# Modulation products in four row bands of one bank, late transposes of the last token tiles, and a moved norm in a two-layer hybrid step

## The chip, the cores and the metric

The kernel runs on one core of a Trainium2 chip. The metric is the device time of one execution in microseconds (us). One profiled execution gives the page and the trace; three executions give the median.

## The reference

One inference step of a two-layer trunk over 128 context tokens and 512 latent tokens, width 1024. Both groups use the same weights, and each has a conditioning vector of its own (c_ctx and c). Layer 0 mixes tokens by grouped-query attention and a gated delta rule side by side, layer 1 by a Mamba-2 scan. The frame around them is this:

```
mod = silu(cond) @ w_mod[layer] + b_mod[layer]           # 1024 -> 6 x 1024, for both vectors
sh1, sc1, g1, sh2, sc2, g2 = split(mod, 6)
h = rms_norm(x) * norm_mix_g * (1 + sc1) + sh1
y, state = even_mixer(h) if layer == 0 else odd_mixer(h)
x = x + g1 * y
h = rms_norm(x) * norm_mlp_g * (1 + sc2) + sh2
x = x + g2 * (max(h @ w_mlp_in, 0) ** 2) @ w_mlp_out
...
return rms_norm(x) * final_norm_g                         # after both layers; also the new caches and states
```

The modulation is a product of a 1024 x 6144 matrix per layer with only two vectors. In odd_mixer the scan's result is normalised over its 2048 channels (rms_norm with a gain) before the output product.

## The kernel before

The 640 tokens are five tiles of 128: tile 0 is the context, tiles 1 to 4 are latent. A product in full precision is made of three products of split operands (high x high, high x low, low x high), so each weight tile that lands raw is cast to a high part (ScalarE) and a low part (VectorE). `gemm` (L304) gives channels on partitions: 24 matmuls accumulate in a bank. `by_rows` (L330) gives tokens on partitions, in two halves (hm) of 512 output columns; the second half holds its last weights back and finishes one token tile after another, calling done(t) after each.

**Modulation.** Shift and scale of layer 0's mixer come first (`mod_first`, product at L515): the weights' 512 columns are cut in four, and four matmuls of 128 columns write to the partitions 0 to 31, 32 to 63, 64 to 95 and 96 to 127 of one bank. The other 20 blocks of 512 columns go through the generator `mod_steps`: it loads a raw tile of 1 MB (two per block, L469) and works on the tile that was loaded one step earlier, so that a caller takes a step wherever it wants one.

- Blocks 4 to 9 of layer 0 (gate g1, shift sh2, scale sc2) run in `delta_in` of the first delta head, three steps ahead of each of four convolution products (12 steps of work). Each k multiplies the [128, 32] window `condst` (the two vectors in columns 0 and 1, zeros behind) by 512 columns into rows 0 to 31 of the bank (L462).
- The other 14 blocks (g2 of layer 0 and all of layer 1) run as `side` of the first MLP: VectorE and ScalarE form the weighted sums in two `macc` tiles (L486, L489), and TensorE adds over the partitions with two products against a selector `msel`, again through L462.

At the end of each block `mod_out` adds the bias to two rows (L444), for some blocks applies 1 + scale and the gain, and writes the rows to a table `modr` in memory, from which `bands` later reads them broadcast to all partitions. `mod_bias` loads the bias and gain rows of each block through SP's queue.

**Norm and transposes.** `modulated` works while the second half of `by_rows` finishes its tiles. Its squares go to ScalarE; done(1), done(2) and done(4) take the root for the tiles that are ready and make the scaled rows `hrow` (L402, L403); `turned` transposes four 128 x 128 pieces of a row tile into a bank (L409) and splits the result into high and low parts (ScalarE L412, VectorE L413). After tile 4, done makes all the transposes that are left, so that in the program they stand ahead of the products that follow: the first `stage` of an MLP, or the scan's first products (`odd`). `stage` takes pairs of weight blocks, and for each half of the tokens (hf) runs four gemms, one for each of four weight tiles j. hf = 0 reads token tiles 0, 1 and the first half of 2.

**The scan's norm.** In `odd` 15 products against the column `stat` (`stc`, L1413) sum the squares of the scan's result, VectorE makes the root `yr`, and the eviction of the output products (`gated`, L365) multiplies by it. These products stand ahead of the output products.

Each engine works through its own queue in order. The order in a queue follows the program where nothing else is said, and the framework may place an instruction later or earlier by a plan of its own (in the trace some products pass transposes that stand ahead of them in the program). Loads of weights go through SP's queue in one sequence.

Of the kernel before, what the change touches and what calls it, by code (L numbers as in the profile page):

```python
# [11 lines left out]
F32 = mybir.dt.float32  # L12
# [99 lines left out]
def _rows(i):  # L112

    out, index, pos = [], {}, 0

    def put(key, v):
        nonlocal pos
        index[key] = pos
        out.append(np.asarray(v).reshape(-1))
        pos += out[-1].size  # L120

    for layer in range(2):
        for c in range(12):
            put(("bias", layer, c), np.stack([i["b_mod"][layer, c * 512:c * 512 + 512]] * 2))
        for c in (2, 3, 8, 9):
            gain = i["norm_mix_g" if c < 4 else "norm_mlp_g"][layer]
            put(("gain", layer, c), np.stack([gain[c % 2 * 512:c % 2 * 512 + 512]] * 2))
    put("gfin", i["final_norm_g"])
    return np.concatenate(out), index
# [36 lines left out]
def _consts():  # L166
# [11 lines left out]
    put("ident", np.eye(P))  # L178
    put("stat", np.full((P, 1), 1.0 / 32.0))
# [28 lines left out]
class Prog:  # L208
    def __init__(self, nc, tc, ctx, io, widx, ridx, pidx, cidx, csmall, taps=None):
        self.nc, self.tc, self.ctx, self.io = nc, tc, ctx, io  # L210
        self.turn, self.share = 0, False
        self.behind = None
        self.mlast = None
        self.widx, self.ridx, self.pidx, self.cidx, self.csmall = widx, ridx, pidx, cidx, csmall
        self.taps = taps or {}
# [91 lines left out]
    def stage(self, keys, xs, half, evac, side=None):  # L307

        for i in range(0, len(keys), 2):
# [9 lines left out]
    def by_rows(self, keys, parts, evac, done=None, side=None, pre=()):  # L319
# [12 lines left out]
        for hm in range(2):  # L332
            banks, held = [], []
            for i, key in enumerate(keys(hm)):
# [3 lines left out]
                for j in range(2):  # L338
# [51 lines left out]
    def modulated(self, pool, scale, shift, h, off, halves):  # L390
# [24 lines left out]
        def done(t):  # L415
# [15 lines left out]
    def mod_bias(self, layer, c, pool):  # L431

        out = []
        for key in ("bias", "gain")[:2 if (layer, c) in self.gains else 1]:
            x = pool.tile([2, 512], F32, name=f"m{key}", tag=f"m{key}", bufs=2 if key == "bias" else 1)
            o = self.ridx[key, layer, c]
            self.nc.sync.dma_start(out=x, in_=self.io["rows"][o:o + 1024].rearrange("(p x) -> p x", p=2))
            out.append(x)
        return out

    def mod_out(self, layer, c, ps, row, gain=None):

        nc = self.nc
        nc.vector.tensor_tensor(out=row, in0=ps[0:2], in1=row, op=ALU.add)  # L444
        if gain is not None:
            nc.vector.scalar_tensor_tensor(out=row, in0=row, scalar=1.0, in1=gain, op0=ALU.add, op1=ALU.mult)
        nc.scalar.dma_start(out=self.modr[layer][c // 2, :, c % 2 * 512:c % 2 * 512 + 512], in_=row)

    def mod_steps(self, todo, landing, small, pool=None, after=None):
# [4 lines left out]
        if pool:  # L454
            sel = pool.tile([P, 2, 32], F32, name="msel")
            nc.vector.memset(sel, 0.0)
            for j in range(2):
                nc.vector.memset(sel[:, j, j:j + 1], 1.0)
        raws, n = [], 2 * len(todo)
# [1333 lines left out]
```

## Time and profile before

| what | value |
|---|---|
| median of 3 runs | 2224.25 us (2221.36 to 2229.6) |
| the profiled execution | 2224.19 us, of which the span of the trace is 2222.4 us |
| TensorE (PE) busy | 2112.9 us, 95% of the span |
| VectorE (DVE) busy | 1386.5 us, 62% |
| ScalarE (ACT) busy | 897.9 us, 40% |
| GpSimd (POOL) busy | 151.1 us, 7% |
| DMA | 232.97 MB, mean 105 GB/s |

Busy time of an engine is an average over stages with different limits. The rows further down are from four views: the page of the whole execution; windows, which give each engine's busy time, the granted TensorE clock (PEclk, 1.00 is 2.4 GHz and 0.50 is 1.2 GHz) and the DMA's share for a stretch; the chain of waits that ended last; and the timeline of one engine. L462 is line 462 of the kernel before, PEld is TensorE's weight load, and x8 means that eight instructions stand in one entry. A product of f32 operands is two instructions in the trace.

### The profile page before, as it was taken

The page shows a single profiled execution, that of the slowest core. Times are in us where ns is not written, and L with a number is a line of the kernel's source. Part 1 is how long each engine was busy: PE and PEld are TensorE (multiplying, and loading weights), DVE is VectorE, ACT ScalarE, POOL GpSimd, SP SyncE. Part 2 cuts the span into 40 slices and gives each one's busy share as a digit, 9 for nine tenths or more (in the row PEclk, how much of TensorE's full clock was granted, in tenths as well). Part 3 has the DMA queues.
Part 4 walks back from the last instruction along what each step waited for, and adds up shares of the span by engine and source line. Part 5 has one row for each costly group of instructions (what it writes and reads, how often), then busy time and mean ns, then how long its engine had stood idle before and what let it go on. Part 6 is the DMA issues. An engine that isn't in the chain of part 4 may idle for free.

```text
span 2222.4 us, 32146 instructions
## 1 busy us (share of the span) xinstructions
PE 2112.9 (95%) x12883; PEld 1851.6 (83%) x12883; DVE 1386.5 (62%) x2606; ACT 897.9 (40%) x1892; POOL 151.1 (7%) x112
## 2 busy tenths in 40 slices
PE   6999789998989999999889999999989799999998
PEld 5958687786787888889789999999968698989896
DVE  6355676766589767574667877777642644444445
ACT  4324435345243322313237876667532231313131
POOL 1031220300000000000000101111210000000000
PEclk9999889999999999999989999999989899999999
DMA  7251100004245434332214443333342121212221
GB/s 316 95 190 64 37 1 17 18 1 149 93 152 211 168 133 145 122 133 79 88 46 151 146 145 115 127 119 113 111 173 83 67 95 57 89 63 81 72 76 48
DMA packets 55152, 232.97 MB, mean 105 GB/s; under 512 B 6487, under 2 KB 20799, under 8 KB 33115
## 3 DMA queue, kind: packets, MB, share of 16 engines
q1 hardware_dynamic: 45192, 216.34, 27.6%
q10 hardware_dynamic: 9810, 14.58, 1.9%
q8 instruction: 101, 1.65, 0.3%
q14 instruction: 49, 0.39, 0.1%
HBM read 222.47 MB, written 8.43 MB: 104 GB/s over the span
## 4 chain that ended last, share of the span: by engine, by line
PE 90%; DVE 5%; DMA 2%; ACT 2%; issue 1%; POOL 0%; SPq 0%; DVEq 0%; ACTq 0%; POOLq 0%
PE gps L304 42%; PE rps L330 28%; PE modps L462 3%; PE yps L1695 2%; PE atps L749 2%; PE avps L1326 2%; PE offps L1709 1%; PE stps L1726 1%; DMA X<-growd 1%; PE scps L1268 1%; DMA wraw<-wall 1%; PE dps L1027 1%; PE dps L1033 1%; PE xkps L1545 1%; PE hps L409 1%
## 5 line engine op out<-in xcount | busy, mean ns | idle before, releaser
L304 PE MATMUL gps<-hh,whi 128*128 128x322 f32 (+3 forms) x1552 | 492.4, 318 | 3.3 <-ACT whi L276 2.6
L304 PE MATMUL gps<-hl,whi 128*128 128x322 f32 (+3 forms) x1552 | 487.0, 314 | 0.0
L304 PE MATMUL gps<-hh,wlo 128*128 128x322 f32 (+3 forms) x1552 | 486.0, 314 | 0.0
L304 PEld LDWEIGHTS gps<-hh,whi 128*128 128x128 f32 (+1 forms) x1552 | 293.5, 189 | 18.4 <-issue 7.6
L304 PEld LDWEIGHTS gps<-hl,whi 128*128 128x128 f32 (+1 forms) x1552 | 293.4, 189 | 6.5 <-issue 5.9
L304 PEld LDWEIGHTS gps<-hh,wlo 128*128 128x128 f32 (+1 forms) x1552 | 293.0, 189 | 3.2 <-issue 2.5
L330 PE MATMUL rps<-wlo,hidh 128*128 128x512 f32 x640 | 253.0, 395 | 0.0
L330 PE MATMUL rps<-whi,hidh 128*128 128x512 f32 x640 | 252.3, 396 | 0.0
L330 PE MATMUL rps<-whi,hidl 128*128 128x512 f32 x640 | 251.5, 395 | 0.0
L276 ACT CAST whi<-wraw 128x1024 fp32r<-128x1024 f32 (+2 forms) x132 | 140.0, 1062 | 259.0 <-PE rps L330 178.9
L304 PE MATMUL gps<-yh,whi 128*128 128x320 f32 x1024 | 227.6, 311 | 1.4 <-DVE yh L413 1.4
L288 DVE TENSOR_TENSOR wlo<-wraw,whi 128x1024 fp32r<-128x1024 f32 x88 | 108.9, 1240 | 189.8 <-ACT whi L287 189.7
L279 DVE TENSOR_TENSOR wlo<-wraw,whi 128x1024 fp32r<-128x1024 f32 (+3 forms) x123 | 156.8, 1276 | 106.4 <-ACT whi L276 105.7
L287 ACT CAST whi<-wraw 128x1024 fp32r<-128x1024 f32 x88 | 91.7, 1048 | 276.2 <-PE rps L330 199.3
L304 PEld LDWEIGHTS gps<-yh,whi 128*128 128x128 f32 x1024 | 173.3, 190 | 2.1 <-DVE yh L413 1.8
L304 PE MATMUL gps<-yh,wlo 128*128 128x320 f32 x512 | 159.3, 311 | 0.0
L330 PEld LDWEIGHTS rps<-whi,hidh 128*128 128x128 f32 x640 | 120.2, 188 | 33.4 <-ACT macc L489 4.2
L330 PEld LDWEIGHTS rps<-whi,hidl 128*128 128x128 f32 x640 | 120.2, 188 | 29.0
L330 PEld LDWEIGHTS rps<-wlo,hidh 128*128 128x128 f32 x640 | 120.3, 188 | 28.5
L649 DVE TENSOR_SCALAR hr<-gps 128x320 f32<-128x320 f32 x128 | 62.4, 488 | 119.9 <-PE gps L304 119.9
L486 DVE SCALAR_TENSOR_TENSOR macc<-wraw,condst,macc 128x512 f32<-128x512 f32 x196 | 136.3, 737 | 0.9 <-DMA wraw<-wall 0.7
L650 ACT ACTIVATE hr<-hr 128x320 f32<-128x320 f32 x128 | 59.9, 469 | 166.8 <-DVE hr L649 166.8
(428 smaller groups left out, 3629.7 us busy)
## 6 DMA issues: line engine op xcount, KB each, us to landing
wraw<-wall SPq DMA_DIRECT2D x158, 1024.0 KB
bc<-afs SPq DMA_DIRECT2D x40, 512.0 KB
Q<-afr SPq DMA_DIRECT2D x64, 128.0 KB
xt<-xt ACTq DMA_DIRECT2D x1, 2560.0 KB
X<-growd SPq DMA_DIRECT2D x8, 320.0 KB
x<-x ACTq DMA_DIRECT2D x1, 2560.0 KB
xd<-x ACTq DMA_DIRECT2D x1, 2560.0 KB
x<-xd SPq DMA_DIRECT2D x1, 2560.0 KB
```

Source lines behind the costliest of these rows:

```text
L276: self.nc.scalar.copy(out=hi, in_=raw[:, :, c:c + m])
L279: eng.tensor_tensor(out=lo, in0=raw[:, :, c:c + m], in1=hi.bitcast(F32), op=ALU.subtract)
L287: self.nc.scalar.copy(out=hi, in_=x)
L288: self.nc.vector.tensor_tensor(out=lo, in0=x, in1=hi.bitcast(F32), op=ALU.subtract)
L304: self.nc.tensor.matmul(ps, ws[k // KT][q // 2][:, k % KT, :], xs[q % 2][k][:, c], start=k == 0 and q == 0, stop=k == n - 1 and q == 2)
L330: nc.tensor.matmul(ps, parts[x][k][:, c], w[y][:, j, :], start=k == 0 and q == 0, stop=k == n - 1 and q == 2)
L462: nc.tensor.matmul(ps, lhs, x, start=start, stop=stop)
L486: nc.vector.scalar_tensor_tensor(out=a, in0=x, scalar=w, in1=a, op0=ALU.mult, op1=ALU.add)
L649: nc.vector.tensor_scalar(out=r, in0=ps, scalar1=0.0, scalar2=None, op0=ALU.max)
L650: nc.scalar.activation(out=r, in_=r, func=AF.Square)
L749: nc.tensor.matmul(ps[:, :n], x[k][:, TOFF[t]:TOFF[t] + P], w[:, k, :], start=k == 0 and q == 0, stop=k == KT - 1 and q == 2)
L1326: nc.tensor.matmul(acc, val(c, i), p, start=c == 1, stop=c == 6)
```

## The change

- **Products side by side.** `mod_steps` cuts the 512 columns in four as `mod_first` does: four products of 128 columns to four groups of 32 partitions. `condst` has the two vectors in columns 32 and 34 of 64, and the window that a block takes of it puts its results into rows of its own. All blocks of a group therefore add up in one bank: a group starts it once and stops it once. The groups are chunks 2 to 4 of layer 0, chunk 5 of layer 0, and all six chunks of layer 1.
- **One way out per group.** `mod_out` runs once per group: an add of the bias, a multiplication by the gains, and four DMAs on ScalarE's queue. The `band` array (bias and gain in the bank's layout) is loaded once per group in place of the rows of each block. `macc` has one buffer for each of its two tiles.
- **Late transposes.** done(4) keeps the transposes of tiles 3 and 4. `stage` makes them after the products j = 1 (one), 2 (one) and 3 (two) of its first pair's first half; the scan makes all four after its first three products, in banks of `ps_x`. `hrow` moves to the weight pool with four buffers. In the even layer the shift rows lie in four tiles that the delta heads used, filled by four loads.
- **The scan's norm.** The 15 products and the root become `mid`, which `by_rows` calls after the products of its first half and ahead of their evictions.
- The final norm's gain is an input array of its own.

```diff
@@ by_rows, stage
             for hf in range(2):
                 for j, w in enumerate(tiles):
                     evac(2 * i + j, hf, self.gemm(w, xs, hf, half))
+                    if i == hf == 0:
+                        self.late((0, 1, 1, 2)[j])
...
+            if mid and not hm:
+                mid()
             for t in range(NT):
                 ps = banks[t] if banks else self.pg.tile([P, 512], F32, name="rps", tag="g")
@@ modulated
-                y = halves(t, j)
+                y = self.wp.tile([P, 512], F32, name="hrow", tag="hrow", bufs=4)
...
-                v.tensor_tensor(out=y, in0=y, in1=shift[:, q, c], op=ALU.add)
+                v.tensor_tensor(out=y, in0=y, in1=shift(q, j), op=ALU.add)
...
-            ps = self.pn.tile([P, 512], F32, name="hps", tag="n")
+            ps = self.bank("hps")
...
-            if t == 4:
-                while todo:
-                    turned(*todo.pop(0))
+            self.turns = todo, turned
...
+    def late(self, n):
+
+        todo, turned = self.turns
+        for _ in range(min(n, len(todo))):
+            turned(*todo.pop(0))
+
+
+    def mod_out(self, layer, chunks, ps, band):
+
+        v = self.nc.vector
+        t = self.small.tile([P, P], F32, name="modt", tag="modt")
+        v.tensor_tensor(out=t, in0=ps, in1=band[:, :P], op=ALU.add)
+        v.scalar_tensor_tensor(out=t, in0=t, scalar=self.cst("scales"), in1=band[:, P:], op0=ALU.add, op1=ALU.mult)
+        r = slice(4 * chunks[0], 4 * chunks[-1] + 4)
+        for q in range(4):
+            self.nc.scalar.dma_start(out=self.modr[layer].rearrange("a b (h q c) -> q (a b h) c", h=2, q=4)[q, r], in_=t[32 * q + r.start:32 * q + r.stop])
@@ mod_steps
         def product(lhs, x, start, stop):
-            nc.tensor.matmul(ps, lhs, x, start=start, stop=stop)
+            for q in range(4):
+                nc.tensor.matmul(ps[32 * q:32 * q + 32], lhs, x[:, q * P:(q + 1) * P], start=start, stop=stop)
...
-                if i % 2 == 0:
-                    nextrows = self.mod_bias(layer, c, small)
...
+                    if first:
+                        ps = self.pmod.tile([P, 512], F32, name="modps", tag="mod")[:, :P]
+                        band = small.tile([P, 2 * P], F32, name="band", tag="band")
+                        nc.sync.dma_start(out=band, in_=self.io["band"][layer])
+                    acc = [pool.tile([P, 512], F32, name="macc", tag=f"macc{j}") for j in range(2)] if pool else []
...
-                        product(self.condst[:, k, :], x, k == 0, k == KT - 1)
+                        product(self.condst[:, k, 32 - row:64 - row], x, first and k == 0, last and k == KT - 1)
...
-                        product(sel[:, j], a, j == 0, j == 1)
-                    self.mod_out(layer, c, ps, *rows)
+                        r = row + 2 * j
+                        product(sel[:, 32 - r:64 - r], a, first and j == 0, last and j == 1)
+                    if last:
+                        self.mod_out(layer, cs, ps, band)
@@ even
-        shift = self.bands(np_.tile([P, 2, D], F32, name="shift"), 0, 3)
+        shift = {}
+        for n, tag in enumerate(("dq1", "dq2", "dq3", "dz3")):
+            q, j = divmod(n, 2)
+            shift[q, j] = ev2.tile([P, PC], F32, name="shift", tag=tag)[:, :512]
+            nc.sync.dma_start(out=shift[q, j], in_=self.modr[0][3, q:q + 1, j * 512:j * 512 + 512].to_broadcast([P, 512]))
@@ odd
             first = [(x, self.gemm(x, xs, 0, HP, cols=CCUT[0])) for x in w]
+            self.bank = lambda name: self.ps_x.tile([P, 512], F32, name=name, tag="x")
+            self.late(4)
...
+            def mid():
+
+                pc = self.bank("stc")
+                for t in range(NT):
+                    for j, y in enumerate([ysq] + sq):
+                        nc.tensor.matmul(pc[:, t:t + 1], y[:, t * P:(t + 1) * P], self.cst("stat"), start=j == 0, stop=j == 2)
...
+            self.by_rows(lambda hm: [("outo", hm, kq) for kq in range(4)], (hh, hl), evac, done, pre=pre, mid=mid)
```

## Rows read from the trace of the kernel before

**Rows 1.** The page, busy time by engine and the chain by engine.

```profile
PE 2112.9 (95%) x12883; PEld 1851.6 (83%) x12883; DVE 1386.5 (62%) x2606; ACT 897.9 (40%) x1892; POOL 151.1 (7%) x112
...
PE 90%; DVE 5%; DMA 2%; ACT 2%; issue 1%; POOL 0%; SPq 0%; DVEq 0%; ACTq 0%; POOLq 0%
```

**Rows 2.** Windows: us, busy us (instructions) by engine, PEclk, DMA share, GB/s.

```profile
28.60:30.50 1.90, 1.90 (x37) 1.39 (x29) 1.90 (x7) 1.90 (x6) 0.00 (x0) 0.50 1.01 418
36.70:38.70 2.00, 2.00 (x67) 1.79 (x66) 1.66 (x12) 0.00 (x0) 0.00 (x0) 1.00 1.02 426
100.00:180.00 80.00, 80.00 (x345) 44.60 (x344) 49.73 (x97) 22.07 (x64) 18.11 (x18) 1.00 0.44 159
110.00:131.00 21.00, 21.00 (x92) 12.38 (x91) 18.13 (x27) 3.85 (x7) 10.99 (x10) 1.00 0.53 188
632.00:1100.00 468.00, 468.00 (x2488) 399.49 (x2487) 326.17 (x514) 144.63 (x237) 0.00 (x0) 1.00 0.38 135
546.00:556.00 10.00, 5.88 (x17) 4.64 (x18) 8.28 (x11) 5.24 (x6) 0.00 (x0) 0.57 0.78 306
1126.00:1132.00 6.00, 5.96 (x23) 4.87 (x24) 2.21 (x2) 1.13 (x3) 0.00 (x0) 0.55 0.41 147
1633.00:1637.00 4.00, 4.00 (x12) 3.14 (x11) 3.94 (x6) 1.04 (x1) 1.56 (x1) 0.57 0.38 162
```

**Rows 3.** The chain of waits: start us, us, engine and line, instructions.

```profile
102.55 3.55 PE modps L462 x8
106.10 1.98 PE gps L304 x12
...
111.62 3.88 PE gps L304 x25
...
743.51 1.83 PE modps L462 x4
...
1628.83 3.02 PE stc L1413 x28
```

**Rows 4.** Timeline of PE, opening: start us, us, engine, line, operation, tiles [idle before].

```profile
28.62 1.93 PE L515 MATMUL modps<-wraw,condst 128*32 128x128 f32 x32
...
36.75 1.95 PE L515 MATMUL modps<-wraw,condst 128*32 128x128 f32 x64
```

**Rows 5.** The chain of waits at a weight load, 1612 to 1620 us.

```profile
1613.45 4.99 DMA wraw<-wall
```

**Rows 6.** Timeline of PE at the first head's transposes.

```profile
139.12 0.27 PE L865 MATMUL kvps<-con,dq 128*128 128x128 f32 x1
```

**Rows 7.** Timeline of DVE, 110 to 131 us.

```profile
111.66 0.68 DVE L444 TENSOR_TENSOR mbias<-modps,mbias 2x512 f32<-2x512 f32 x1 [0.76 <-PE modps L462]
...
130.23 0.82 DVE L678 SCALAR_TENSOR_TENSOR vt<-cb,vt 128x642 f32<-128x642 f32 x1
```

**Rows 8.** Timeline of PE at a wait in the even layer's output products.

```profile
550.12 2.50 PE L330 MATMUL rps<-whi,op 128*128 128x512 f32 x5 [4.19 <-ACT whi L287]
```

**Rows 9.** Timeline of PE ahead of the second MLP.

```profile
1747.78 1.94 PE L409 MATMUL hps<-con,hrow 128*128 128x128 f32 x8 [7.12 <-DVE hrow L403]
...
1754.47 1.94 PE L409 MATMUL hps<-con,hrow 128*128 128x128 f32 x8 [4.75 <-DVE hrow L403]
...
1760.32 0.90 PE L304 MATMUL gps<-yh,whi 128*128 128x320 f32 x2 [1.40 <-DVE yh L413]
```

**Rows 10.** Timeline of DVE ahead of the second MLP.

```profile
1750.31 0.16 DVE L243 SCALAR_TENSOR_TENSOR nr<-rsa,nr 128x2 f32<-128x2 f32 x1
1750.39 0.68 DVE L413 TENSOR_TENSOR yh<-hps,yh 128x512 fp32r<-128x512 f32 x1
```

**Rows 11.** Timeline of PE ahead of the scan.

```profile
1123.59 0.66 PE L409 MATMUL hps<-con,hrow 128*128 128x128 f32 x4 [1.40 <-DVE hl L413]
...
1125.87 0.64 PE L304 MATMUL gps<-hh,whi 128*128 128x322 f32 x1 [1.62 <-ACT whi L276]
```

**Rows 12.** Timeline of DVE at the evictions of the odd layer's output products.

```profile
1680.74 1.45 DVE L365 SCALAR_TENSOR_TENSOR rps<-rps,yr,gate 128x512 f32<-128x512 f32 x2 [1.85 <-PE rps L330]
```

More of the change, by code (lines that the diff above doesn't have):

```diff
@@ L109, in _stream, with _bands, band @@
     return np.concatenate(out), index
[L112 to L129, printed above, removed]
+def _bands(i):
+    def band(rows):
+        x = np.stack(rows, axis=0).reshape(6, 2, 4, P)
+        o = np.zeros((4, 8, 2, 2, P), np.float32)
+        o[:, :6] = x.transpose(2, 0, 1, 3)[:, :, None]
+        return o.reshape(P, P)
+    one = np.ones(D, np.float32)
+    return np.stack([np.concatenate([
+        band(list(i["b_mod"][layer].reshape(6, D))),
+        band([one, i["norm_mix_g"][layer], one, one, i["norm_mlp_g"][layer], one])], axis=1) for layer in range(2)])
 def _params(i):
@@ L388, in norm_rows, with modulated @@
         return square, root
-    def modulated(self, pool, scale, shift, h, off, halves):
+    def modulated(self, pool, scale, shift, h, off):
         nc, v = self.nc, self.nc.vector
@@ L535, in setup @@
         self.modr = [self.dr.tile([6, 2, D], F32, name=f"modr{l}") for l in range(2)]
-        self.gains = {(l, c) for l in range(2) for c in (2, 3, 8, 9)}
         npr = self.io["prm"].shape[1]
@@ L795, in even @@
         np_, self.pn, self.pg = self.pools(e1, ("mn0", 1, "left"), ("pn1", 2, None), ("pg2", 6, None))
+        self.bank = lambda name: self.pn.tile([P, 512], F32, name=name, tag="n")
         h = [hp.tile([P, KT, PC], F32R, name=n) for n in ("hh", "hl")]
@@ L818, in even @@
                 e1, ("on0", 1, "right"), ("hid0", 1, "left"), ("mraw", 2, "left"), ("pn2", 1, None), ("pmod2", 1, None), ("pg3", 6, None))
-            side = self.mod_steps([(0, 10), (0, 11)] + [(1, c) for c in range(12)], mraw, np_, hid, lambda: self.mlast)
+            side = self.mod_steps([(0, (5,)), (1, range(6))], mraw, np_, hid, lambda: self.mlast)
             next(side)
@@ L827, in late @@
                 self.padding(np_, h)
-                square, done = self.modulated(np_, scale, shift, h, TOFF, lambda t, j: hid.tile([P, 512], F32, name="hrow", tag="macc", bufs=4))
+                square, done = self.modulated(np_, scale, lambda q, j: shift[:, q, j * 512:j * 512 + 512], h, TOFF)
                 sq.append(square)
@@ L1388, in odd @@
             self.pn, self.pg, np_ = self.pools(e1, ("pn3", 2, None), ("pg5", 6, None), ("on1", 1, "right"))
+            self.bank = lambda name: self.pn.tile([P, 512], F32, name=name, tag="n")
             sq = [np_.tile([P, NTOK], F32, name="ysq", tag=f"ysq{j}") for j in range(2)]
@@ L1408, in odd @@
                     nc.vector.scalar_tensor_tensor(out=hl[k], in0=y, scalar=sc, in1=hh[k].bitcast(F32), op0=ALU.mult, op1=ALU.subtract)
-            pc = self.pn.tile([P, 512], F32, name="stc", tag="n")
-            for t in range(NT):
-                for j, y in enumerate([ysq] + sq):
-                    nc.tensor.matmul(pc[:, t:t + 1], y[:, t * P:(t + 1) * P], self.cst("stat"), start=j == 0, stop=j == 2)
-            ym, yr = (np_.tile([P, NT], F32, name=n, tag=n) for n in ("ym", "yr"))
-            nc.vector.tensor_scalar(out=ym, in0=pc[:, :NT], scalar1=16.0 / D, scalar2=EPS, op0=ALU.mult, op1=ALU.add)
-            self.rsqrt(np_, yr, ym, [P, NT])
             self.x = xp.tile([P, NT, D], F32, name="x")
@@ L1420, in odd @@
             shift, scale = (self.bands(np_.tile([P, 2, D], F32, name=f"band{kind}"), 1, kind) for kind in (3, 4))
-            square, done = self.modulated(np_, scale, shift, h, [P * t for t in range(NT)],
-                                          lambda t, j: np_.tile([P, 512], F32, name="hrow", tag="hrow", bufs=4))
+            square, done = self.modulated(np_, scale, lambda q, j: shift[:, q, j * 512:j * 512 + 512], h, [P * t for t in range(NT)])
             def evac(t, hm, ps):
@@ L1762, in prepare @@
     arrays = {
-        "wall": wall, "rows": rows, "prm": prm, "cst": cst,
+        "wall": wall, "gfin": i["final_norm_g"], "band": _bands(i), "prm": prm, "cst": cst,
         "x": x.reshape(NT, P, D).transpose(1, 0, 2),
```

66 lines of the change are left out of this document (26 added, 40 removed).

## The prediction

> **What bounds the kernel now.** I read the page first, then the windows, then the chain, then the timeline of single engines. The page says TensorE: it is busy for 95% of the span and holds 90% of the chain that ended last [rows 1]. The windows say where it is the bound without a gap: in 100 to 180 us and in 632 to 1100 us its busy time equals the length of the stretch, at full clock, while VectorE has room [rows 2]. Any TensorE work taken out of these two stretches should come off the end, as long as nothing else is close behind. The chain then shows what sits between the wide products there: the modulation's products, eight instructions of 3.55 us at a time in the delta stage and four of 1.83 us in the MLP [rows 3]. Where TensorE does stand idle I read the timeline of TensorE and VectorE around the gap.
>
> The profiled execution took 2224.19 us with a span of 2222.4 us; the median of three is 2224.25 us. I work from 2224.2 us, so the 1.8 us around the span stays.
>
> **Part 1, products side by side.** Before, a block's product is a [128, 32] stationary operand against 512 columns, two instructions each. The chain's x8 and x4 are one step of the delta stage, which has 12, and one block of the MLP, which has 14 [rows 3]. After, each becomes four products of 128 columns, one per 32 partitions of the bank. The opening of this kernel already runs that form: at the full level (2.4 GHz) 64 instructions take 1.95 us, 0.030 us each, and at the half level (1.2 GHz) 32 take 1.93 us, 0.060 us each [rows 2, 4]. A 512-column instruction takes 3.55/8 = 0.444 us. Four 128-column ones in 0.12 us mean the four quarters really overlap.
> - Delta stage: a step becomes 32 instructions, 32 x 0.030 = 0.97 us, plus 0.1 us that I allow for entering and leaving (an estimate). It saves 3.55 - 1.07 = 2.48 us, times 12 = 29.8 us of TensorE time.
> - MLP: a block becomes 16 instructions, 0.48 + 0.1 = 0.58 us for 1.83, so 1.25 us times 14 = 17.5 us.
>
> A rule speaks against this. The Trainium skill (TensorE: Matmul & The Clock Gate, "Wait — 56ns, not 53.3ns?") says that without hardware decode the sequencer spends about 62 ns per matmul. By that a step of 32 would take 1.98 us and a block of 16 0.99 us, and the sum below would end near 2184 us. The full-level row has 30 ns, so the trace doesn't bear the rule out for this form; what it would do is rival 3.
>
> **What of the 29.8 us arrives.** Three things could wait once TensorE is faster.
> (a) The raw weights. Tile i+2 is requested when step i ends; its step starts after two runs of wide products and one step, 1.98 + 1.07 + 3.88 = 6.9 us [rows 3]. A 1 MB load took 4.99 us from issue to use [rows 5]. So it stays hidden, by 1.9 us.
> (b) VectorE's in-order queue. TensorE transposes the first head's q, k and v at 139.12 us [rows 6]. The last of its inputs, vt, comes from VectorE at 130.23 + 0.82 = 131.05 us [rows 7]. VectorE has been busy for 18.13 of the 21 us up to there [rows 2], mostly with the attention's preparation, which doesn't get shorter; it loses only two mbias adds of about 0.7 us and a wait of 0.76 us [rows 7], about 2.1 us. So vt is ready at 128.9. Six steps lie ahead of the transposes, so TensorE arrives at 139.1 - 6 x 2.48 = 124.2 and waits 4.7 us, if the order of its queue stays.
> (c) The clock. Around an idle time of 4.19 us the mean granted clock of 10 us was 0.57, with 5.88 us of work in them [rows 2, 8]. The waiting itself I have counted; the work after it runs at half speed, so a wait of this size would cost about another 2.7 us (half of some 5.4 us of work).
> Net: 29.8 - 4.7 - 2.7 = 22.4 us. The bounds are 29.8 (the queue is arranged around the wait) and 7.5 (the second six steps, 14.9 us, are given back as well).
>
> In the MLP VectorE is busy 326 of 468 us [rows 2] and 14 blocks in 468 us leave 33 us for each one's sums; I take all 17.5 us, at the least 14 (three blocks' gain lost at the ends of the four hidden blocks). That the accumulators (macc) have one buffer each instead of two sets costs nothing: the step that issues a block's product comes before the one that starts the next block's sums in the program, so the new write waits for a product that takes 0.6 us.
>
> Writing out once per group and not per block removes 17 of 20 small adds of 0.68 us [rows 7] and 17 bias loads, and turns 20 writes into 12. All of it is off TensorE, so nothing for the sum. It adds a wait: the two band loads of layer 1 now need the group's last product and stand in SP's queue ahead of weight loads. The bands are first needed in the last row products of the MLP; SP loses a few us, under the cover of tiles already landed. I count 0, at most +5.
>
> **Part 2, the last tiles' transposes.** Three places.
> - Before the first MLP: TensorE waits for tile 2, as before the second (below). The change doesn't touch tile 2, and in the timeline the products already pass tiles 3 and 4 here. 0, with 3 us either way because VectorE's order may change.
> - Before the second MLP: the same 7.12 us for tile 2 stays. But here the products come only after tiles 3 and 4: waits of 4.75 and 1.40 us, and transposes of eight instructions in 1.94 us, until 1760.32 [rows 9]. Tile 2's last half is ready at 1750.39 + 0.68 = 1751.1 [rows 10]. So products can start 9.2 us earlier; the 16 transposes come back between them. At full clock eight may take half of 1.94 us, about 1 us (an estimate; no row has them alone at that level), but part of that lies in gaps of wide products; net gain 8 us, between 0 (the order stays) and 9.
> - Before the scan: two waits of 1.40 us, of which the second is shown, and one of 1.62 us at the last tiles go [rows 11], and with them the half level that follows (mean clock 0.55 over 6 us, about 2.7 us of work) [rows 2]: 7.1 us. The last of these waits is for the weights' cast, and its memory may be that of the bands that tile 4 still reads; I take off 1 us. Gain 6 us, between 0 and 10.
>
> **Part 3, the scan's norm behind the products.** At the start it frees 3.02 us [rows 3] and a half level after it, 1.7 us of work (mean 0.57 over 4 us, all of them busy) [rows 2]: 4.7 us. It returns behind the first half's products: 15 sums of two instructions, as long as before, 3.0 us; then VectorE makes the root, 12 operations, 0.16 us each for two columns [rows 10] and 0.2 us for five with the steps between them (an estimate), 2.4 us, and only then can it evict: 0.73 us (1.45 for two) [rows 12] and an add that takes 0.68 us [rows 10], 1.4 us per tile. TensorE has one free bank, five tiles at 0.7 us, and waits for four evictions behind the root: 2.4 + 4 x 1.4 - 4 x 0.7 = 5.2 us. Before, the first eviction overlapped the last products. Net +3.7, rounded to a loss of 4 us, between -5 (the sums slip into gaps) and +10 (the half level follows).
>
> The shift rows now come by four loads into tiles of the delta heads, so two of them wait for the last head. If SP held the first output weights behind them, 4 to 8 us would be lost; I count 0, as the framework may issue the loads in another order.
>
> **Sum.** 2224.2 - 22.4 - 17.5 - 8 - 6 + 4 = 2174.3 us; forecast 2174.
>
> **The rivals.**
> 1. The delta stage gives back the second half as well, to waits on VectorE and the attention's start: 14.9 us less gain, 2189. For it: what releases the attention's start is not TensorE alone, and a queue in program order moves a wait on rather than ending it. Against: over the whole of 100 to 180 us VectorE has 30 us free, most of them after 131 us [rows 2]. 0.2.
> 2. Everything carries: no wait at the transposes (7.4 us more) and the norm costs nothing but its own time or less (6 us): 2161. For it: the timeline shows products passing what isn't ready. 0.2.
> 3. The narrow instructions are bound by their number and cost 0.060 us each, as in the half-level row [rows 4], because weight loads between wide products hold them up. A step takes 1.93 + 0.1 us and saves 1.52, times 12 = 18.2; a block takes 0.97 + 0.1 and saves 0.76, times 14 = 10.6; the lead at the transposes is 6 x 1.52 = 9.1 us, about what vt allows. 2224.2 - 18.2 - 10.6 - 8 - 6 + 4 = 2185. Against: the full-level row [rows 4]. 0.05. The Trainium skill's rule of part 1 is of this kind.
> 4. Slower than before: the raw tiles come too late at each of the 12 steps, as weight loads share the queue. It decides from a load of about 6.9 us. If every step then waited 4 us and the clock fell each time (another 2.6 us), that would be 12 x 6.6 = 79 us against the 29.8 us of shorter work: 2224.2 + 79 - 29.8 - 17.5 - 8 - 6 + 4 = 2246. Against: the load of 4.99 us. 0.03.
> 5. The gains of parts 2 and 3 cancel and part 1 is hardly seen, within 0.5%: 0.02.
>
> **How the numbers follow.** The forecast has 0.5. The range has to hold rivals 1 to 3 in part: rival 2 and a little below gives 2158, rival 1 and a little above 2193. A measurement of this kernel tells about 0.5% (11 us) from no change; every case but the last two is faster by more. Faster 0.94, same 0.03, slower 0.03.
>
> **What would show it.** Steps of 32 modulation instructions at about 1.05 us, blocks of 16 at 0.6 us; a TensorE wait on VectorE near the first head's transposes; no waits for hrow between the 7 us gap and the second MLP's products; a new wait for VectorE in the middle of the odd layer's output products, about 1640 us into the span. Wrong would be: steps near 2 us (rival 3), TensorE waiting for raw tiles in the delta stage (rival 4), or other stages, which the change doesn't touch, moving by more than 5 us.

## The result and the profile after

The changed kernel takes 2153.2 us (median of 4 runs, 2148.23 to 2154.41) where the kernel before takes 2226.93 us (4 runs, 2221.36 to 2236.16): a ratio of 0.9661, 95% interval 0.9623 to 0.9698. That is 74 us, where 50 us were forecast, and 5 us below the low end of the range. The profiled execution took 2148.23 us with a span of 2146.4 us, 76.0 us less than the one before.

The page of the changed kernel, beside [rows 1]:

```profile
PE 2054.9 (96%) x13339; PEld 1846.3 (86%) x13339; DVE 1373.3 (64%) x2585; ACT 898.4 (42%) x1892; POOL 153.4 (7%) x112
...
PE 89%; DVE 7%; DMA 3%; ACT 1%; issue 1%; DVEq 0%; SPq 0%; ACTq 0%
```

TensorE lost 58.0 us of busy time (2112.9 to 2054.9) and the span 76.0 us, so 18 us of idle time went as well. It is still the bound.

Where the time went is read by pairing: each VectorE and ScalarE instruction whose name stands equally often in two traces is compared with its namesake of the same number, and the median of the differences in a stretch says how far ahead the one kernel is there. The steps of that lead, in us against the profiled execution before (a plus is a gain; the kernels in the last three columns are explained below; each entry is rounded by itself, so a column can miss its sum by 0.1):

| stage (us in the kernel before) | forecast | changed | e_side | no_late | no_mid |
|---|---|---|---|---|---|
| opening (0 to 95) | 0 | +1.2 | -0.1 | +0.9 | +1.1 |
| delta stage (95 to 210) | +22.4 | +29.1 | +29.1 | +29.1 | +29.1 |
| delta heads and attention, to the first output products (210 to 580) | 0 | +7.5 | +4.1 | +7.2 | +7.5 |
| first MLP (580 to 1075) | +17.5 | +16.6 | +18.9 | +18.3 | +16.5 |
| to the end of the scan (1075 to 1535) | +6 | +6.6 | -2.3 | +3.6 | +7.5 |
| output products of layer 1 (1535 to 1720) | -4 | +5.6 | +0.7 | +6.3 | +4.1 |
| to the second MLP (1720 to 1850) | +8 | +9.6 | +2.8 | +0.1 | +9.9 |
| sum | 49.9 | 76.1 | 53.2 | 65.5 | 75.7 |

The attention's entry moves by itself: a repeat of the changed kernel has +9.9 us there in place of +7.5, and the eight traces in which TensorE's order there is that of the changed kernel have +4.1 to +10.0 (the last section). In the other stages the repeat differs from the first trace by 1.2 us at most.

So three terms are off: the delta stage by 6.7 us, the attention by 7.5 us, the output products of layer 1 by 9.6 us. The other four are right within 2 us.

In the delta stage, the timeline of TensorE in the changed kernel (start, duration, line, operation, count, idle time before and its releaser):

```profile
117.48 1.08 PE L459 MATMUL modps<-wraw,condst 128*32 128x128 f32 x32
...
121.65 0.27 PE L870 MATMUL kvps<-con,dq 128*128 128x128 f32 x1
121.76 0.27 PE L870 MATMUL kvps<-con,kt 128*128 128x128 f32 x1
...
124.21 1.08 PE L459 MATMUL modps<-wraw,condst 128*32 128x128 f32 x32 [0.54 <-DMA wraw<-wall]
...
126.75 1.08 PE L459 MATMUL modps<-wraw,condst 128*32 128x128 f32 x32
128.51 0.44 PE L870 MATMUL kvps<-con,vt 128*128 128x128 f32 x2 [0.68 <-DVE vt L679]
```

VectorE's last operation on vt:

```profile
127.31 1.14 DVE L679 SCALAR_TENSOR_TENSOR vt<-cb,vt 128x642 f32<-128x642 f32 x1
```

A step takes 1.08 us (3.55 before, [rows 3]). vt is ready at 127.31 + 1.14 = 128.45 us, near the forecast's 128.9, but the wait for it is 0.68 us and not 4.7: the queue was laid out anew. In the kernel before the transposes of q, k and v stand together (q's are in [rows 6], v's follow 0.2 us later); here q and k go from 121.4 us on, and two modulation steps, some wide products and transposes of the attention's keys fill the time until vt is there.

In the output products of layer 1, TensorE and VectorE behind the first half's products:

```profile
1613.71 2.73 PE L1436 MATMUL stc<-con,ysq 128*128 128x1 f32 x24
...
1623.69 0.50 PE L328 MATMUL rps<-whi,yh 128*128 128x512 f32 x1 [0.17 <-ACT rps L381]
```

```profile
1616.48 0.17 DVE L1437 TENSOR_SCALAR ym<-stc 128x5 f32<-128x5 f32 x1 [0.27 <-PE stc L1436]
...
1618.90 3.39 DVE L365 SCALAR_TENSOR_TENSOR rps<-rps,yr,gate 128x512 f32<-128x512 f32 x5
1622.21 3.07 DVE L366 TENSOR_TENSOR x<-x,rps 128x512 f32<-128x512 f32 x5
```

The root takes 2.4 us and the evictions follow, as forecast. But TensorE idles 0.17 us and not 5.2: in the one free bank it runs 30 products of the second half for a single tile, one k after the other (some 7 us), before it turns to the next tile.

Ahead of the second MLP (against [rows 9]) the first wide product comes straight behind tile 2's transposes:

```profile
1681.35 1.94 PE L409 MATMUL hps<-con,hrow 128*128 128x128 f32 x8 [7.12 <-DVE hrow L403]
1683.11 1.70 PE L300 MATMUL gps<-yh,whi 128*128 128x320 f32 x5
```

### The profile page after: what moved, and what is told of

It is laid out like the page before. It is cut to its first block, busy times and chain, and to the rows that moved or that the text cites. A ratio compares the mean times of both kernels' runs of the same rounds, so it can differ in the third digit from the quotient of the medians.

```text
span 2146.4 us, 32954 instructions
## 1 busy us (share of the span) xinstructions
PE 2054.9 (96%) x13339; PEld 1846.3 (86%) x13339; DVE 1373.3 (64%) x2585; ACT 898.4 (42%) x1892; POOL 153.4 (7%) x112
## 4 chain that ended last, share of the span: by engine, by line
PE 89%; DVE 7%; DMA 3%; ACT 1%; issue 1%; DVEq 0%; SPq 0%; ACTq 0%
PE gps L300 41%; PE rps L328 28%; PE atps L750 2%; PE yps L1704 2%; PE avps L1331 2%; DMA wraw<-wall 1%; PE offps L1718 1%; PE dps L1038 1%; PE stps L1735 1%; PE scps L1273 1%; DMA X<-growd 1%; PE dps L1032 1%; PE xkps L1554 1%; PE modps L459 1%; PE scps L1303 1%
```

## The experiments

Theory A, formed after the result: TensorE's queue is laid out anew by the framework's plan when the instructions change, and ready work is moved into waits; TensorE time that is taken out then comes off whole, and waits worked out from the order of before don't arise. The rival is the forecast's own premise that the order stays. A second rival for single stages is that the buffers that the change moved (hrow, the shift rows) did it.

| kernel | median us (runs) | before beside it | ratio, 95% interval |
|---|---|---|---|
| mlp_only | 2206.54 (4) | 2231.49 (7) | 0.9907 (0.9873 to 0.9941) |
| e_side | 2168.43 (4) | 2231.49 (7) | 0.9725 (0.969 to 0.976) |
| no_mid | 2151.65 (4) | 2231.49 (7) | 0.965 (0.9624 to 0.9676) |
| no_late | 2157.88 (4) | 2231.49 (7) | 0.9679 (0.9653 to 0.9706) |
| hrow_norm_pool | 2163.66 (4) | 2224.88 (7) | 0.9714 (0.9682 to 0.9746) |
| pin_att | 2158.93 (4) | 2224.88 (7) | 0.9697 (0.9662 to 0.9732) |
| pin_mid | 2157.81 (4) | 2224.88 (7) | 0.9687 (0.9653 to 0.9721) |
| pin_kv | 2146.83 (4) | 2224.88 (7) | 0.9638 (0.9609 to 0.9667) |
| after_again | 2151.38 (5) | 2230.83 (11) | 0.9648 (0.962 to 0.9677) |
| late_odd | 2149.09 (5) | 2230.83 (11) | 0.9645 (0.9618 to 0.9673) |
| late_odd_kv | 2149.62 (6) | 2230.83 (11) | 0.965 (0.9622 to 0.9678) |

Totals tell some 7 us apart; below that the pairing of the traces is used, stage by stage. The traces come from several chips, so a difference between two of them has to be larger than what the repeat of the changed kernel shows.

**mlp_only**: the kernel before with a second generator that has the narrow products, used by the MLP alone.

```diff
...
-            side = self.mod_steps([(0, 10), (0, 11)] + [(1, c) for c in range(12)], mraw, np_, hid, lambda: self.mlast)
+            side = self.mod_steps2([(0, (5,)), (1, range(6))], mraw, np_, hid, lambda: self.mlast)
```

> The kernel before, with the products side by side and the one way out per group in the first MLP alone; the delta stage keeps its wide products and its 20-block loop's first six blocks as before. Theory A (TensorE time that is taken out comes off the end whole, and TensorE's queue in the delta heads and the attention is laid out anew only when the stage ahead of it changes): 16.5 us faster than before, all of it between 600 and 1010 us, and the stage from 250 to 546 us as long as before (the order of its instructions on TensorE is that of before). Theory B (the gain of 7.5 us at the end of the attention stage comes from elsewhere than the delta stage's products): 24 us faster. If the narrow products are bound by their number (0.060 us each): 10.6 us faster.

Measured: a lead of -0.8 us at 580 us and of +17.5 us at 1075 us, so 18.2 us in the MLP, and nothing gained in the attention stage (-1.0). The total (0.6 to 1.3% faster, 13 to 28 us) excludes the 10.6 us, if barely, but does not tell 16.5 from 24; the pairing does. Theory A holds here, and the narrow products are not bound by their number.

**e_side**: the changed kernel with transposes, shift rows, hrow, macc and the norm as before.

```diff
-                y = self.wp.tile([P, 512], F32, name="hrow", tag="hrow", bufs=4)
+                y = halves(t, j)
...
             self.turns = todo, turned
+            if t == 4:
+                self.late(9)
...
-            self.by_rows(lambda hm: [("outo", hm, kq) for kq in range(4)], (hh, hl), evac, done, pre=pre, mid=mid)
+            self.by_rows(lambda hm: [("outo", hm, kq) for kq in range(4)], (hh, hl), evac, done, pre=pre)
```

> Part 1 alone: products side by side in the delta stage and the MLP and one way out per group; transposes, shift rows, hrow, macc and the scan's norm as before. Theory A (the queue is laid out anew; nothing waits for vt, and the attention stage gets another order): 30 us in the delta stage, 7.5 us in the attention stage, 16.5 us in the MLP, together 54 us faster than before. My forecast's theory (the order of the queue stays): 22.4 + 17.5 = 40 us faster. If the 7.5 us come from the shift rows or hrow: 46 us.

Measured: 53.2 us between the two profiled executions, 2.75% (2.4 to 3.1%, some 61 us) by the ratio; the forecast's 40 us (1.8%) are excluded. The delta stage gives 29.1 us and the attention stage 4.1 us. TensorE's queue holds the products of the delta heads and the attention in one and the same order in e_side and in the changed kernel, and in another one in the kernel before and mlp_only, which gains nothing there. So the order comes with the change to the modulation in the delta stage, not with the buffers.

**pin_att**: the changed kernel with the old place of the attention's scores.

```diff
-                nc.tensor.matmul(pk[:, i * P:(i + 1) * P], kT[:, t, :], qT[:, TOFF[t]:TOFF[t] + P], start=True, stop=True)
+                m = nc.tensor.matmul(pk[:, i * P:(i + 1) * P], kT[:, t, :], qT[:, TOFF[t]:TOFF[t] + P], start=True, stop=True)
+                if h == 0:
+                    self.pin = m
...
-                        nc.tensor.matmul(out, x[:, i, t * P:(t + 1) * P], kst[q][:, kv, k0:k1], start=q == 0, stop=q == 1)
+                        with self.tc.issue_after(self.pin.ins):
+                            nc.tensor.matmul(out, x[:, i, t * P:(t + 1) * P], kst[q][:, kv, k0:k1], start=q == 0, stop=q == 1)
```

> The changed kernel, with the attention's score products held behind the delta head 0's product of k and q, where they stood in the kernel before (there TensorE idled 12.8 us at 266 to 279 us). No instruction is added or taken away. Theory A (the shorter attention stage comes from the order in TensorE's queue, which fills this wait with scores): TensorE idles 10 to 13 us there, and the stage from 227 to 508 us is 5 to 10 us longer. Rival (the scores only come back later, in other gaps): within 2 us of the changed kernel at 508 us.

The longest waits of TensorE at this place, in the kernel before, in the changed kernel and in pin_att:

```profile
263.48 0.48 PE L865 MATMUL kvps<-con,dq 128*128 128x128 f32 x1 [4.05 <-DVE dv L870]
279.32 2.05 PE L971 MATMUL dps<-dq,kT 128*128 128x128 f32 x8 [12.81 <-DVE M L950]
```

```profile
233.10 0.45 PE L870 MATMUL kvps<-con,dq 128*128 128x128 f32 x1 [5.33 <-ACT qs L1264]
...
245.63 0.50 PE L1273 MATMUL scps<-kst,qs 128*128 128x512 f32 x1 [1.35 <-DVE mx L1280]
```

```profile
234.70 0.45 PE L871 MATMUL kvps<-con,dq 128*128 128x128 f32 x1 [5.58 <-ACT qs L1267]
243.22 2.47 PE L977 MATMUL dps<-dq,kT 128*128 128x128 f32 x10 [3.98 <-DVE M L956]
...
254.84 1.44 PE L955 MATMUL dps<-kT 128*128 128x128 f32 x5 [4.97 <-ACT kT L939]
```

In pin_att the wait for M is 3.98 us in place of the scores, and another of 4.97 us follows: not the 10 to 13 us expected in one piece. Its lead over the changed kernel goes from -1.4 us ahead of the stage to -7.8 us behind it, so the stage is 6.4 us longer. That is most of what the stage had gained (7.5 us).

The idle time of the whole stage says it without the clock. Its windows in the three kernels, ends set by the pairing (us, busy us by engine, clock, DMA share, GB/s):

```profile
210.00:580.00 370.00, 333.29 (x2148) 282.92 (x2147) 246.17 (x626) 161.21 (x409) 58.06 (x43) 0.92 0.14 46
```

```profile
179.70:542.20 362.50, 334.09 (x2148) 285.70 (x2147) 245.87 (x625) 161.62 (x409) 52.48 (x38) 0.92 0.14 47
```

```profile
181.00:550.00 369.00, 330.96 (x2148) 283.71 (x2147) 241.72 (x626) 162.47 (x409) 52.42 (x38) 0.92 0.15 46
```

TensorE idles 36.7 us before, 28.4 in the changed kernel and 38.0 in pin_att, with as many instructions. In the eight traces with the changed kernel's order it is 27.2 to 30.7 us.

**pin_kv**: z and the left modulation steps held behind the first transposes.

```diff
-        list(islice(mods, 3))
+        list(islice(mods, 1))
         self.conv_silu(tp, vt, w[0], xs, cw[:, 8 + h, :], None)
-        list(islice(mods, 3))
-        self.silu2(tp, dn["z"], w[1], xs)
-        list(mods)
...
+                kv = nc.tensor.transpose(pt[:, i * P:(i + 1) * P], x[:, c], self.ident)
+            if t == 0:
+                with self.tc.issue_after(kv.ins) if h == 0 else nullcontext():
+                    list(islice(mods, 3))
+                    self.silu2(tp, dn["z"], w[1], xs)
+                    list(mods)
```

> The changed kernel, with the gate products (z) of the first delta head and the modulation's steps that are then left held behind the first tile's transposes of q, k and v. No instruction is added or taken away. My forecast's theory (these transposes wait for vt and what stands behind them waits as well): TensorE idles 4 to 5 us near 120 us, and with the lower clock behind it the delta stage is 5 to 8 us longer than in the changed kernel. Rival (vt is ready before TensorE comes to it): 0. What the attention stage does after it is open, since its order is laid out anew.

```profile
113.57 1.08 PE L459 MATMUL modps<-wraw,condst 128*32 128x128 f32 x32 [0.71 <-DMA wraw<-wall]
116.52 1.93 PE L459 MATMUL modps<-wraw,condst 128*32 128x128 f32 x32 [1.87 <-DMA wraw<-wall]
120.56 0.42 PE L1185 MATMUL ktps<-con,akl 128*64 128x128 f32 x1 [1.54 <-DVE akl L1180]
124.88 0.48 PE L1184 MATMUL ktps<-con,akl 128*128 128x128 f32 x1 [1.60 <-ACT kst L1188]
```

The delta stage is 8.9 us longer: 5.7 us of waits in four pieces, and half the clock behind them (1.93 us for a step of 1.08). So an order that holds work back behind these transposes does cost time, and the rival's 0 is out. The size is near the forecast's (4.7 + 2.7 = 7.4), but that does not confirm the forecast's working. None of the four waits is put down to vt: two are for raw tiles, as the steps now come closer together, and two for VectorE and ScalarE in the attention's key transposes; v's first transpose follows at 125.86 us without a gap. And with z held back TensorE is at the transposes of q and k already at 111.82 us, 14 us ahead of v's.

But the attention stage, in a third order, is 11.4 us shorter than in the changed kernel (11.3 in late_odd_kv, below), and the total doesn't show the loss at all. Of these 11.4 us TensorE's idle time is 2.2 (26.2 for 28.4 us); the rest is busy time (324.9 for 334.1 us) at a mean granted clock of 0.95 in place of 0.92. A loss in a stage can thus be outweighed in the next.

**no_mid**: the norm ahead of the products again.

```diff
...
-            self.by_rows(lambda hm: [("outo", hm, kq) for kq in range(4)], (hh, hl), evac, done, pre=pre, mid=mid)
+            self.by_rows(lambda hm: [("outo", hm, kq) for kq in range(4)], (hh, hl), evac, done, pre=pre)
```

> The changed kernel with the scan's norm back ahead of the output products. Theory A (behind the products of the first half the norm costs TensorE nothing but its own time, since the one free bank takes a whole tile's products in the meantime): 6 us slower than the changed kernel. My forecast's theory (the root and the evictions hold TensorE up): 4 us faster than the changed kernel. If the 4 us less idle time at the start of these products came from an earlier weight load and not from the norm: 2 us slower or less.

Measured: the total is that of the changed kernel, the gain of this stage 4.1 in place of 5.6 us. So the norm's move is worth between nothing and 1.5 us. The forecast's loss of 4 us is wrong, and so is theory A's gain of 6 us: some four of the 5.6 us come from elsewhere.

**pin_mid**: the second half's products held in the written order.

```diff
...
-                nc.tensor.matmul(ps, parts[x][k][:, c], w[y][:, j, :], start=k == 0 and q == 0, stop=k == n - 1 and q == 2)
+                with self.tc.issue_after(prev[0].ins) if prev else nullcontext():
+                    m = nc.tensor.matmul(ps, parts[x][k][:, c], w[y][:, j, :], start=k == 0 and q == 0, stop=k == n - 1 and q == 2)
+                if mid and chain[0]:
+                    prev[:] = [m]
...
+                chain[0] = True
```

> The changed kernel, with the products of the second half of layer 1's output stage in the order in which the program writes them (for each k all five token tiles), each behind the one before. My forecast's theory for the norm: TensorE has one free bank and runs into four evictions that wait for the root, a wait of about 5 us behind the 15 sums and half the clock for 2 to 3 us after it: 5 to 8 us slower than the changed kernel. Rival (the evictions keep up all the same): within 1 us of it.

```profile
1612.79 1.70 PE L1441 MATMUL stc<-con,ysq 128*128 128x1 f32 x14
...
1621.73 0.80 PE L330 MATMUL rps<-whi,yh 128*128 128x512 f32 x1 [6.42 <-ACT rps L386]
```

A wait of 6.42 us, and half the clock behind it (window: us, busy us by engine, clock, DMA share, GB/s):

```profile
1621.70:1626.00 4.30, 4.27 (x10) 3.44 (x11) 1.61 (x3) 2.43 (x8) 0.00 (x0) 0.50 0.32 112
```

What the wait is made of, on VectorE and then on ScalarE:

```profile
1616.94 3.39 DVE L370 SCALAR_TENSOR_TENSOR rps<-rps,yr,gate 128x512 f32<-128x512 f32 x5
1620.24 3.07 DVE L371 TENSOR_TENSOR x<-x,rps 128x512 f32<-128x512 f32 x5
```

```profile
1620.96 0.60 ACT L386 ACTIVATE rps<-x 128x512 f32<-128x512 f32 x1 [7.96 <-DVE x L371]
```

The lead over the changed kernel falls from +2.2 to -6.7 us, 9.0 us in all. The forecast's wait (5.2 us) is thus near for an order that the queue does not have, but its parts are others. It let TensorE wait for four evictions of one tile each. Here it is one wait, for the first bank: all five multiplications come ahead of the first add, and the bank is free only after ScalarE's square for the norm has used it, a step that the forecast left out.

**hrow_norm_pool**: no_late with hrow of layer 1 in the norm's pool.

```diff
...
-                y = self.wp.tile([P, 512], F32, name="hrow", tag="hrow", bufs=4)
+                y = (hp or self.wp).tile([P, 512], F32, name="hrow", tag=tag, bufs=4)
...
-            square, done = self.modulated(np_, scale, lambda q, j: shift[:, q, j * 512:j * 512 + 512], h, [P * t for t in range(NT)])
+            square, done = self.modulated(np_, scale, lambda q, j: shift[:, q, j * 512:j * 512 + 512], h, [P * t for t in range(NT)], np_)
```

> The kernel no_late with one edit: the scaled rows of the layer 1 MLP's norm (hrow) lie in the norm's own pool again, as in the kernel before, and not in the weights' pool. No instruction is added or taken away. Theory C (with hrow in it the weights' pool lies on memory that comes free earlier, so the casts of the first output weights of layer 1 no longer wait): the idle time ahead of these products goes back from 4.4 to 8.4 us, and the run is 4 to 6 us slower than no_late, all of it at 1550 to 1560 us. Rival (the shorter wait there comes from the norm's move or from chance): within 1 us of no_late.

TensorE's first output product and ScalarE's queue ahead of it, in no_late and then in hrow_norm_pool:

```profile
1557.12 0.57 PE L328 MATMUL rps<-whi,yh 128*128 128x512 f32 x1 [4.06 <-ACT yh L1413]
1554.44 1.99 ACT L283 CAST whi<-wraw 128x1024 fp32r<-128x1024 f32 x2 [4.04 <-DVE yt L1541]
1556.34 2.60 ACT L1413 CAST yh<-yt 128x640 fp32r<-128x640 f32 x4
```

```profile
1564.78 0.79 PE L328 MATMUL rps<-whi,yh 128*128 128x512 f32 x1 [8.00 <-ACT yh L1413]
1554.03 3.87 ACT L283 CAST whi<-wraw 128x1024 fp32r<-128x1024 f32 x4
1563.06 1.04 ACT L283 CAST whi<-wraw 128x1024 fp32r<-128x1024 f32 x1 [5.16 <-DMA wraw<-wall]
1564.01 2.60 ACT L1413 CAST yh<-yt 128x640 fp32r<-128x640 f32 x4
```

The wait is 8.00 us again (7.39 in the kernel before, 4.06 in the changed one), and this stage is 4.7 us longer by the pairing. (Another 2 to 3 us are lost at 275 us and 1.4 us in the scan, where the two programs are alike; see the last section.) The size is as expected, the mechanism isn't: no cast comes earlier with hrow in the weights' pool. With it there ScalarE has two casts ahead of the scan's result yh; without it, four, and then a fifth that waits 5.16 us for a raw tile, and yh stands behind it. The traces of before and e_side, which also have hrow in the norm's pool, show the same four and a fifth; those of the changed kernel and no_mid show the two. Where a buffer lies changed how many casts the plan could put ahead.

**no_late**: the transposes of tiles 3 and 4 ahead of the products again.

```diff
             self.turns = todo, turned
+            if t == 4:
+                self.late(9)
```

> The changed kernel with the last tiles' transposes back ahead of the next products, in all three places; shift rows and hrow stay as changed. The ledger of the two traces gives the part 6.3 us before the scan and 9.7 us before the second MLP: 16 us slower than the changed kernel. My forecast: 6 + 8 = 14 us. If the move of hrow to other memory and not the order were the cause: 0 to 5 us.

Measured against the changed kernel, stage by stage: 1.8 us gained at the first MLP, 2.9 us lost before the scan and in it, 9.6 us lost before the second MLP, 10.6 us in all between the traces. Between the medians of no_late and no_mid, from one chip, it is 6.2 us. The expected 16 us are too many. In front of the second MLP the row of before is back:

```profile
1689.01 1.94 PE L409 MATMUL hps<-con,hrow 128*128 128x128 f32 x8 [4.75 <-DVE hrow L403]
...
1694.86 0.90 PE L300 MATMUL gps<-yh,whi 128*128 128x320 f32 x2 [1.40 <-DVE yh L413]
```

Before the scan it is not: no_late still gains 3.6 us there where e_side loses 2.3. The rows of ScalarE that cast the scan's first weights, in e_side and in no_late, show why:

```profile
1072.65 0.59 ACT L412 CAST hh<-hps 128x512 fp32r<-128x512 f32 x1 [1.47 <-PE hps L409]
1073.13 1.99 ACT L272 CAST whi<-wraw 128x1024 fp32r<-128x1024 f32 x2
```

```profile
1061.06 1.99 ACT L272 CAST whi<-wraw 128x1024 fp32r<-128x1024 f32 x2 [1.40 <-DVE hrow L403]
```

As long as hrow lies in the MLP's memory, the weights of the next stage are cast behind the last transpose that reads it; with hrow in the weights' pool they are cast 12 us earlier in the span, of which 3.5 us are the lead that no_late has here anyway (the table), and products fill the waits between the transposes. e_side and no_late differ in other buffers too, so that it is hrow alone is read from these rows and not shown by a run with that edit only, which was not tried.

**late_odd, late_odd_kv and after_again**: the changed kernel with the first MLP's transposes early, this together with pin_kv, and the changed kernel once more.

```diff
-                    if i == hf == 0:
+                    if i == hf == 0 and not side:
                         self.late((0, 1, 1, 2)[j])
...
+            if t == 4 and flush:
+                self.late(9)
...
```

> The changed kernel as it is, beside the next two on the same chip: about 73 us faster than before (2153 us where before takes 2226).

> The changed kernel, with the last tiles' transposes ahead of the products again in front of the first MLP only; the scan and the second MLP keep them late. The trace of no_late was 1.8 us ahead of the changed kernel's just there: 1.8 us faster than the changed kernel by 640 us of the span, which a total may not show. If that difference came from the clock's level and not from the order: 0.

> late_odd and pin_kv together. In pin_kv the delta stage was 8.9 us longer and the attention stage behind it, in another order, 11.4 us shorter than in the changed kernel. If that order of the attention stage carries over (its order on TensorE is the same here): 4 us faster than the changed kernel, 2149 us against 2153. If it was the clock's phase in that one run: the same as the changed kernel or up to 5 us slower.

late_odd has the 1.8 us: its lead over the changed kernel goes from 1.0 to 2.75 us at the first MLP. late_odd_kv has 2.4 us there, and 11.3 us in the attention. In the totals all three are the same within 2.3 us on one chip, and their intervals overlap. None of the versions tried beats the changed kernel by what can be measured.

## Why the prediction was wrong, step by step

The step that failed is one premise, used in three places, that TensorE's queue keeps the order of before; beside it a term was put at nothing without a reason (hrow).

- **Narrow products.** Right. 1.08 us for a step (forecast 1.07), 29.1 us in the delta stage (gross 29.8), 18.2 us in mlp_only (17.5). The row of the opening [rows 4] was the right price, and rival 3 is out: 32 instructions in 1.08 us are 0.034 us each. The Trainium skill gives some 62 ns per matmul with hardware decode off (TensorE: Matmul & The Clock Gate, "Wait — 56ns, not 53.3ns?"). No run here shows whether it was on; at 0.034 us each these instructions were not bound so.
- **"If the order of its queue stays" (b, c).** This failed, and it cost 6.7 us of the sum. vt's time was forecast rightly (128.9 us, 128.45 measured), but the queue was laid out anew, and the stage has two waits of 0.68 and 0.54 us in place of 4.7 us and a lower clock behind them. That a held order costs something of this size (8.9 us in pin_kv) is shown, not that the forecast's 7.4 us were its right price. The condition stood in the text and got no chance of its own but for rival 2.
- **Delta heads and attention.** The sum had no term for a stage that the change doesn't touch, and rival 1 looked for a loss there. It gained 7.5 us, because the attention's scores now fill a wait of 12.8 us: TensorE's idle time in the stage falls by 8.3 us, and pin_att gives all of it back. A stage that moves by over 5 us untouched is what the prediction itself named as a sign of being wrong.
- **The norm.** Forecast -4, measured 0 to +1.5. The same premise failed: the five-tile order behind the one free bank was the written one, and only pin_mid, which holds it, has the wait (6.42 us, made of other parts than the forecast's 5.2). Without the wait the forecast's own terms give 4.7 - 3.0 = +1.7. (With it they give 3.0 + 5.2 - 4.7 = 3.5 us of loss, not the 3.7 written.)
- **hrow.** The move to the weights' pool was costed at nothing, unmentioned in the sum. It is worth some 4 us at the output products of layer 1 (shown by hrow_norm_pool) and, argued from the rows above, part of the 6.6 us up to the scan's end. There the forecast of 6 us was right in size and only partly in reason: without the late order 3.6 us of it remain.
- **Late transposes.** Before the second MLP right: 8 us forecast, 9.6 measured, all of it gone in no_late. Before the first MLP the forecast of 0 missed a loss of 1.8 us, inside its bounds.
- **Raw tiles, band loads, shift rows.** No loss shows: in the delta stage TensorE's one wait for a raw tile is the 0.54 us above, and no wait of TensorE behind the opening ends with a band or a shift row.
- **The range.** Its low end let every forecast wait vanish at once but no stage win something new. The bounds of the norm (a gain of 5) and the scan (a gain of 10) reached below it and were not added.

## What to carry to other kernels

Where a framework lays out the queues by a plan, price work on the bound engine by what it takes, and treat a wait worked out from the old order as one of two cases, with the other at zero: ready work is moved into it where there is any and where a bank or a buffer lets it. Count a buffer's new place as an edit: it decides which casts and loads the plan can put ahead of which. Here a stage behind the change became 1 to 19 us shorter than before by a new order and the clock that came with it; before crediting an edit with a total, pair the two traces stage by stage, and read idle and busy time apart.

## What the runs showed of the hardware

The clock behind a wait is not the same in each run of a program. From 260 to 300 us of their spans the changed kernel, its repeat, and e_side (whose products there are in the same order) have nearly the same busy time and other clocks:

```profile
260.00:300.00 40.00, 38.77 (x231) 33.15 (x231) 30.21 (x68) 15.71 (x35) 7.65 (x6) 0.87 0.00 1
```

```profile
260.00:300.00 40.00, 38.77 (x250) 33.08 (x249) 32.45 (x73) 17.43 (x38) 8.17 (x6) 0.93 0.00 1
```

```profile
260.00:300.00 40.00, 38.78 (x209) 33.00 (x207) 27.32 (x53) 15.67 (x33) 8.14 (x6) 0.77 0.00 1
```

The repeat of the changed kernel gains 2.4 us there on its first run, and no_late and hrow_norm_pool, alike in this stage, differ by 2 to 3 us. Over the whole attention stage the eight traces in this one order (the changed kernel, its repeat, e_side, no_mid, no_late, hrow_norm_pool, pin_mid and late_odd) gain 4.1 to 10.0 us on the kernel before; their idle time lies within 3.5 us (27.2 to 30.7), their busy time between 329.4 and 338.1 us. So the difference between 7.5 us (changed) and 4.1 us (e_side) is mostly the clock's (334.1 and 336.9 us busy, 28.4 and 28.9 idle), and the length of a stage behind a long wait is read to some 6 us from one trace. pin_att (+1.1) lies below all eight, pin_kv (+18.8) above.

What e_side gains before the second MLP (2.8 us) is of the same kind. The stage in the kernel before and in e_side:

```profile
1720.00:1850.00 130.00, 116.19 (x637) 105.19 (x636) 67.57 (x130) 39.04 (x66) 0.00 (x0) 0.92 0.22 77
```

```profile
1669.60:1796.80 127.20, 113.39 (x637) 102.50 (x636) 67.52 (x130) 39.03 (x66) 0.00 (x0) 0.95 0.22 79
```

TensorE idles 13.8 us in both, and the same 637 instructions take 2.8 us less at a mean granted clock of 0.95 in place of 0.92. Why the clock is higher there no run shows.
